# First SwiGLU block: the output of the last 1024 inner features as seven-product units whose operands lie in the room of the input's

## Chip, core and metric

The kernel runs on one core of a Trainium2 chip. The metric is the device time of one execution in microseconds (us). The kernel before takes 1906.6 us (median of three runs, 1905.49 to 1906.69). The engines are named as in the profile: PE multiplies matrices, DVE and ACT work on vectors, POOL adds and issues some transfers, SP issues most transfers.

## What is computed

One layer of a streaming encoder on 576 frames (512 of a prompt, 64 of a sample): a SwiGLU block, a mixer of three branches, a second SwiGLU block, and a final norm.

```python
def swiglu(x, w_in, w_out):
    a, b = jnp.split(x @ w_in, 2, axis=-1)
    return (jax.nn.silu(a) * b) @ w_out

def layer(x, lp, st):
    h = x + 0.5 * swiglu(rmsnorm(x, lp['norm_ffn1']), lp['w_ffn1_in'], lp['w_ffn1_out'])
    mix, new_st = mixer(rmsnorm(h, lp['norm_mix']), lp, st)
    h = h + mix
    h = h + 0.5 * swiglu(rmsnorm(h, lp['norm_ffn2']), lp['w_ffn2_in'], lp['w_ffn2_out'])
    return h, new_st
```

The model has 1024 features, a block 4096 inner features, so `w_in` is 1024 x 8192 and `w_out` 4096 x 1024. The change concerns the last 1024 rows of `w_ffn1_out` alone: x += 0.5 * g[:, 3072:4096] @ w_ffn1_out[3072:4096, :].

## The kernel before

Features lie on the 128 partitions, frames along the free axis. A float32 operand is split into a high part in the matrix engine's reduced format (a cast on ACT, line 335) and the rest (a subtraction on DVE, line 336); a product is the sum of three matmuls, high x high, high x low, low x high. High and low are ph and pl for weights, TH and TL for the moving operands of the seven-product form, YH and YL (XH and XL in the mixer) for those of plain products.

**Seven products.** Most of the layer uses one step of Strassen's scheme (Winograd's form) over a unit: 1024 rows of weights in two halves of 512, two output tiles of 128 features, and the frames in two halves of 288. A unit takes seven products instead of eight; one is 4 depth steps x 3 terms = 12 matmuls of 288 columns (`product`, line 714). They are named X1, A11, X3, X4, A22, A21, X2 after their weights. X1, X2, X3, X4 are sums of weight blocks: a transfer from POOL's queue adds two blocks in wx, and POOL adds a third block for X3 and for X4 (line 561). Blocks come as 256 KB tiles wr on SP's queue. Rings limit how far this runs ahead: five wr, four wx, six ph, six pl. `stream` puts out the units one after the other; in the slot of unit n stand X1, A11, X3, X4 of n between A22, A21, X2 of n-1. X1, A22, X3 and X2 of a unit share one accumulator bank, X4 and A21 another, A11 has one for all units; each product is read out of its bank by DVE or ACT before the next on that bank starts.

**The block.** `ffn` takes the inner features in four chunks c of eight tiles j. An input unit (c, j) makes one tile of both halves of `w_in` and turns them into g, 128 x 2 x 288 (`swiglu`, lines 725 to 741). An output unit (c, m) multiplies the g of chunk c with two column tiles of `w_out` and adds the results to the residual x, which is R (`residual`, line 753). Its moving operands are made from pairs of g tiles by `hidden_operands`: seven casts, seven TL and five differences of 288 columns (line 762) for each of four pairs. They stand in T2; the input's own operands stand in T, which has the same size. `tick` hands out one of the pieces at each product.

The order of units is: (0, 4..7); then for c = 1, 2, 3 the input units (c, 0), (c, 1), the four output units of chunk c-1, and (c, 2..7). After the stream the last chunk's output is plain: `hidden_parts` has split its g tiles into YH and YL, and `gemm` multiplies two blocks of 512 rows (i in (6, 7)) with four blocks of 256 columns, frames in halves of 256 and 320 (line 280); the second block does the first 256 frames of most columns before the other 320. Results are added to R at line 812. Then R is stored to `xs`, and the mixer begins: `norm` scales R into XH and XL (lines 392, 393), sums squares (lines 343 to 347), takes the root (line 352) and spreads it into rs with small transposes (line 385); its first plain products use XH and XL, their results are multiplied with rs (line 698), and `operands` makes xk and its differences from R and rs (from line 512).

The order of instructions on each engine is set by the framework's list scheduler, which places what a line emits by readiness in its own model; accumulator reads have a raised priority. Each engine then executes its own list strictly in order.

Of the kernel before, what the change touches and what calls it, by code (L numbers as in the profile page):

```python
# [26 lines left out]
F32 = mybir.dt.float32  # L27
# [6 lines left out]
TP = 512  # L34
HALVES = ((0, 256), (256, 320))
CH = [(0, 128), (128, 128), (256, 128), (384, 128), (512, 64)]
NB = 63
NS = 115
FH = 288
NPLAIN = 4  # L40
BUFS = {"g": 9, "t": 5, "P": 4, "Q": 2, "bias": 2}
# [1 line left out]
FBUFS = {"P": 5, "g": 5, "s": 3}  # L43
# [42 lines left out]
class Hybrid:  # L86
    def __init__(self, ctx, tc, I, O):
        self.tc, self.nc, self.I, self.O = tc, tc.nc, I, O
        self.op = None
        self.stay = {}  # L90
        self.plan = []
        self.splan = []
        self.ahead = {}
        self.steps = None
        self.b_i, self.b_n, self.fetched = 0, 0, deque()
        self.evicted = {}
        self.behind = 0
        self.jobs, self.gap, self.side = deque(), 0, iter(())
        nc = self.nc
        self.const = ctx.enter_context(tc.tile_pool(name="const", bufs=1))  # L100
        self.dram = ctx.enter_context(tc.tile_pool(name="scr", bufs=1, space=bass.MemoryType.DRAM))
        c = self.const
        self.R1 = c.tile([128, 8, T], F32, name="R1")
        self.rs = c.tile([128, T], F32, name="rs")
        self.small = ctx.enter_context(tc.tile_pool(name="small", bufs=8, reuse_waits="tile"))

        self.wt = ctx.enter_context(tc.tile_pool(name="wt", bufs=1, reuse_waits="tile"))
        self.xs = self.dram.tile([128, 8, T], F32, name="xs")

        self.ys = [self.dram.tile([128, T], F32, name=f"ys{i}") for i in range(16)]  # L110
        self.gs = [self.dram.tile([128, T], F32, name=f"gs{i}") for i in range(24)]
        self.scr = self.dram.tile([24, T], F32, name="scr_rows")


    @contextmanager
# [639 lines left out]
                done()  # L755
        return on

    def hidden_operands(self, kk, b1, b2):

        nc = self.nc  # L760
        put = lambda src, t: self.split(src, *(v[:, kk, :] for v in self.T2[t]))
        sub = lambda o, one, two: nc.vector.tensor_tensor(o, one, two, op=ALU.subtract)  # L762
        (b11, b12), (b21, b22) = ((b[:, 0, :], b[:, 1, :]) for b in (b1, b2))
        put(b22, self.T_X1)
        yield 1
        for t, b in ((self.T_A11, b12), (self.T_X3, b11)):
            d = self.P((128, FH))
            sub(d, b, b22)
            put(d, t)
            yield 1  # L770
        put(b11, self.T_X4)
        yield 1
        for t, one, two in ((self.T_A22, b22, b21), (self.T_A21, b12, b11), (self.T_X2, b21, b11)):
            sub(one, one, two)
            put(one, t)
            yield 1
# [5 lines left out]
    def ffn(self, x, g0, win, wout, name, last=(0, 1)):  # L782
# [3 lines left out]
        nc = self.nc  # L786
# [26 lines left out]
            return go  # L813


        def at(c, j):
            return (8 * c + (j if c == 3 else j % 2 * 4 + j // 2)) * 128

        boxes = [{} for _ in range(NPLAIN)]
        tiles = []  # L820
# [27 lines left out]
        def flush():  # L848
# [3 lines left out]
            for c, j in sorted(got):  # L852
                if c == 3:
                    self.jobs.append(self.hidden_parts(j, got.pop((c, j))))
                elif j % 2 == 0 and (c, j + 1) in got:
                    self.jobs.append(self.hidden_operands(j // 2, got.pop((c, j)), got.pop((c, j + 1))))
                    if j == 6:
                        free[0] = False

        def unit(c, j):  # L860
            def done(g):
                got[c, j] = g
                flush()
            return (win, 0, 4096 + at(c, j), at(c, j)), self.T, self.swiglu(done)

        def out(c, m):
            def done():
                free[0] = True
                if c == 2:
                    self.hidden_tiles(name)  # L870
                flush()
            return (wout, 1024 * c, 256 * m, 256 * m + 128), self.T2, self.residual(x, m, done if m == 3 else None)

        for j, box in enumerate(boxes):
            got[0, j] = box["g"]
        flush()
        seq = [unit(0, j) for j in range(NPLAIN, 8)]
        for c in range(1, 4):
            seq += [unit(c, j) for j in range(2)] + [out(c - 1, m) for m in range(4)] + [unit(c, j) for j in range(2, 8)]
        order = ((0, self.T_X1), (1, self.T_A22), (0, self.T_A11), (1, self.T_A21), (0, self.T_X3), (1, self.T_X2),  # L880
                 (0, self.T_X4))
        self.stream(seq, order, lambda n: {self.T_X1: n % 3, self.T_A11: 3, self.T_X4: 4 + n % 2})
        self.drain()
        for i in (6, 7):
            tiles = [((wout, i * 512, 512, j * 256, 256), [(0, evac_o(2 * j)), (128, evac_o(2 * j + 1))])
                     for j in range(4)]
            n = 1 if i == 7 else 4
            self.gemm(tiles[:n], self.YH, self.YL, k0=(i % 2) * 4)
            self.gemm(tiles[n:], self.YH, self.YL, k0=(i % 2) * 4, half_major=True, order=last)
# [692 lines left out]
    def run(self):  # L1582
# [42 lines left out]
        with self.ffn_phase("c"):  # L1625
            self.norm(x, C_G2, self.YH, self.YL)
            self.ffn(x, C_G2, "w_ffn2_in", "w_ffn2_out", "c", last=(1, 0))
            self.norm_out(x, C_GF, (self.O["y0"], self.O["y1"]))
        assert (len(self.plan), len(self.splan)) == (NB, NS), (len(self.plan), len(self.splan))

    def branches(self, x):
# [48 lines left out]

_INS = {"xT": (1024, T), "wblk": (NB, 128, 1024), "sblk": (NS, 128, 2048), "cst": (128, C_N), "bias": (128, 8, 256), "ckT": (512, 512),
        "cv": (512, 512), "s0": (128, 1024), "mc0": (4, 128, 129)}
# [11 lines left out]
def pack(plans, inp):  # L1694
# [11 lines left out]
    w["gate"] = gate  # L1706
    wb = np.empty((NB, 128, 1024), f32)
    for i, (n, r0, nr, c0, ncol) in enumerate(plan):
# [61 lines left out]
```

## Time and profile before

| | |
|---|---|
| median of three runs | 1906.6 us (1905.49 to 1906.69) |
| profiled execution: time, span | 1904.78 us, 1903.0 us |
| granted clock of PE | 0.994 |
| busy: PE, DVE, ACT, POOL | 98%, 81%, 56%, 36% |
| first block's stream, first and last product | about 62 us, 525 us |
| its plain tail, between the stream's end and the mixer's first product | to 574.45 us |

Times in the trace are from the span's start. A row of the profile names the line, the engine, the operation, out<-in by the program's names and the shapes; "idle before" is idle time of that engine just before, with what ended it. A PE row is about 0.3 us long, but rows overlap: what a matmul costs is the time from one start to the next.

### The profile page before, as it was taken

How to read it: one execution, taken by the hardware profiler on the slowest of the kernel's cores; microseconds unless marked ns; L12 is line 12 of the kernel's file. 1: busy time of each engine (PE TensorE's matmuls, PEld its weight loads, DVE VectorE, ACT ScalarE, POOL GpSimd, SP SyncE). 2: the span in 40 equal slices, each digit the busy share in tenths (PEclk: the TensorE clock that was granted, in tenths of full speed). 3: DMA queues.
4: the chain of work that ended last, by engine and by line, in shares of the span. 5: the costliest groups of instructions: out<-in, count | busy, mean ns of one | idle time of the engine just before them, and what ended most of it. 6: DMA issues, size and time to landing. Idle time of an engine off the chain costs nothing. (4 is left out here: it accounts for less than half of the span.)

```text
span 1903.0 us, 37603 instructions
## 1 busy us (share of the span) xinstructions
PE 1860.0 (98%) x13901; PEld 1812.3 (95%) x13901; DVE 1538.0 (81%) x2723; ACT 1070.9 (56%) x2406; POOL 685.6 (36%) x645
## 2 busy tenths in 40 slices
PE   9899999999999899999999999999999999999998
PEld 9899999999999779989899999999999999999997
DVE  7999999998858858767778776655899988889865
ACT  6554654554535677677676675334465554554544
POOL 3443343343301324523535453530344334333311
PEclk9999999999999999999999999999999999999999
DMA  7356666566643455755657655642446656656531
GB/s 222 107 155 167 163 158 173 156 165 167 178 132 111 128 156 157 213 164 132 189 156 188 177 157 187 212 154 75 122 115 167 173 156 166 166 157 169 148 100 56
DMA packets 129439, 294.69 MB, mean 155 GB/s; under 512 B 14288, under 2 KB 26192, under 8 KB 129256
## 3 DMA queue, kind: packets, MB, share of 16 engines
q1 hardware_dynamic: 99368, 203.42, 32.1%
q0 software_dynamic: 20272, 74.20, 20.7%
q10 hardware_dynamic: 9616, 14.69, 2.6%
q8 instruction: 109, 1.79, 0.4%
q14 instruction: 74, 0.61, 0.1%
HBM read 272.87 MB, written 19.38 MB: 154 GB/s over the span
## 5 line engine op out<-in xcount | busy, mean ns | idle before, releaser
L714 PE MATMUL acc<-TH,ph 128*128 128x288 f32 x3220 | 962.4, 300 | 18.4 <-ACT uv L622 5.5
L714 PE MATMUL acc<-TL,ph 128*128 128x288 f32 x3220 | 956.0, 297 | 1.3 <-DVE TL L336 1.1
L714 PE MATMUL acc<-TH,pl 128*128 128x288 f32 x3220 | 949.6, 296 | 0.6 <-DVE pl L336 0.6
L714 PEld LDWEIGHTS acc<-TH,ph 128*128 128x128 f32 x3220 | 605.1, 188 | 33.0 <-ACT uv L622 7.4
L714 PEld LDWEIGHTS acc<-TL,ph 128*128 128x128 f32 x3220 | 606.8, 188 | 5.6 <-issue 2.9
L714 PEld LDWEIGHTS acc<-TH,pl 128*128 128x128 f32 x3220 | 607.8, 189 | 1.8 <-DVE pl L336 1.1
L336 DVE TENSOR_TENSOR pl<-wr,ph 128x512 fp32r<-128x512 f32 x471 | 449.8, 961 | 83.1 <-ACT ph L335 71.4
L335 ACT CAST ph<-wr 128x512 fp32r<-128x512 f32 x471 | 287.5, 618 | 271.6 <-PE acc L714 146.3
L336 DVE TENSOR_TENSOR pl<-wx,ph 128x512 fp32r<-128x512 f32 x390 | 319.3, 822 | 32.6 <-ACT ph L335 26.8
L335 ACT CAST ph<-wx 128x512 fp32r<-128x512 f32 x390 | 237.6, 620 | 181.3 <-POOL wx L561 97.1
L561 POOL TENSOR_TENSOR wx<-wx,wr 128x512 f32<-128x512 f32 x160 | 246.2, 1539 | 179.2 <-DVE pl L336 143.9
L549 POOL DMA_DIRECT2D wx<-in_sblk x115 | 101.4, 915 | 497.9 <-DVE pl L336 186.0
L280 PE MATMUL acc<-YH,ph 128*128 128x256 f32 (+1 forms) x768 | 227.2, 298 | 2.4 <-ACT g L629 2.2
L280 PE MATMUL acc<-YL,ph 128*128 128x256 f32 (+1 forms) x768 | 227.4, 297 | 0.6 <-DVE YL L393 0.6
L280 PE MATMUL acc<-YH,pl 128*128 128x256 f32 (+1 forms) x768 | 227.1, 296 | 0.0
L280 PEld LDWEIGHTS acc<-YH,ph 128*128 128x128 f32 x768 | 145.2, 190 | 3.5 <-ACT g L629 2.3
L280 PEld LDWEIGHTS acc<-YL,ph 128*128 128x128 f32 x768 | 145.5, 189 | 1.1 <-DVE YL L393 1.0
L280 PEld LDWEIGHTS acc<-YH,pl 128*128 128x128 f32 x768 | 145.3, 189 | 0.0
L561 POOL TENSOR_TENSOR wy<-wx,wr 128x512 f32<-128x512 f32 x35 | 62.7, 1793 | 122.1 <-DVE pl L336 100.0
L753 DVE SCALAR_TENSOR_TENSOR R<-acc,R 128x288 f32<-128x288 f32 x168 | 75.7, 451 | 17.3 <-PE acc L714 16.3
L335 ACT CAST TH<-g 128x288 fp32r<-128x288 f32 x120 | 51.4, 433 | 49.5 <-POOL g L739 31.5
L739 POOL TENSOR_TENSOR g<-g,P 128x288 f32<-128x288 f32 x56 | 63.3, 1130 | 40.9 <-ACT P L738 40.8
(325 smaller groups left out, 2348.3 us busy)
## 6 DMA issues: line engine op xcount, KB each, us to landing
wr<-in_sblk SPq DMA_DIRECT2D x345, 256.0 KB, 3.6
wx<-in_sblk POOLq DMA_DIRECT2D x119, 512.0 KB, 6.5
wx<-in_sblk SPq DMA_DIRECT2D x111, 512.0 KB, 3.7
wr<-in_wblk SPq DMA_DIRECT2D x126, 256.0 KB, 3.0
R<-scr_rows ACTq DMA_DIRECT2D x12, 576.0 KB, 6.4
gs<-g SPq DMA_DIRECT2D x20, 288.0 KB, 3.5
g<-gs POOLq DMA_DIRECT2D x20, 288.0 KB, 3.6
y<-ys POOLq DMA_DIRECT2D x12, 288.0 KB, 5.2
```

The costliest lines, as they stand in the source:

```text
L280: last = nc.tensor.matmul(ps[:, :n], wt[:, wsl], xx[:, k0 + k, a:a + n], start=(k == 0 and i == 0), stop=(k == nk - 1 and i == 2))
L335: self.cast = self.nc.scalar.copy(hi, src).ins
L336: self.nc.vector.tensor_tensor(lo, src, hi.bitcast(F32), op=ALU.subtract)
L549: nc.gpsimd.dma_start(x12, src[:, 1:3, :], accum_op=ALU.add)
L561: add = lambda o, one, two: self.nc.gpsimd.tensor_tensor(o, one, two, op=ALU.add)
L714: self.nc.tensor.matmul(ps, wt[:, wsl], xx[:, kk, :], start=(start and kk == 0 and i == 0), stop=(kk == 3 and i == 2), skip_group_check=True)
L739: nc.gpsimd.tensor_tensor(s["g"][:, 1, :], s["g"][:, 1, :], a, op=ALU.mult)
L753: self.nc.vector.scalar_tensor_tensor(o, ps, scale, o, op0=ALU.mult, op1=ALU.add)
```

## The change

For the first block alone (`name == "a"`):

- All eight input units of chunk 3 stand ahead of the output units of chunk 2, and four output units (3, m) stand behind those. The tail of plain products is gone; the second block keeps it.
- The moving operands of chunk 3's output are made by `hidden_operands` too, written into T, when the input units no longer need it. The tiles j of this chunk are renumbered so that the pairs come out right.
- Five g buffers hold the tiles j = 3..7. The first three are stored to DRAM (hs) by SP and loaded back (`again`) when a buffer is free.
- In all, 55 weight blocks of the plain form and 119 of the seven-product form, where it was 63 and 115.

```diff
-    def hidden_operands(self, kk, b1, b2):
+    def hidden_operands(self, kk, b1, b2, to=None):
         nc = self.nc
-        put = lambda src, t: self.split(src, *(v[:, kk, :] for v in self.T2[t]))
+        put = lambda src, t: self.split(src, *(v[:, kk, :] for v in (to or self.T2)[t]))
...
+        seven = name == "a"
         def at(c, j):
-            return (8 * c + (j if c == 3 else j % 2 * 4 + j // 2)) * 128
+            if c == 3:
+                return (24 + ((6, 3, 7, 0, 4, 1, 5, 2)[j] if seven else j)) * 128
+            return (8 * c + j % 2 * 4 + j // 2) * 128
...
+        def again(i):
+            g = self.wp.tile([128, 2, FH], F32, name="g", tag="g", bufs=FBUFS["g"])
+            nc.sync.dma_start(g, self.hs[i])
+            return g
+
+        def last_operands(gs):
+            put = partial(self.hidden_operands, to=self.T)
+            yield from put(0, gs[0], gs[1])
+            g0, g1 = again(0), again(1)
+            yield from put(1, gs[2], gs[3])
+            g2 = again(2)
+            yield from put(2, gs[4], g0)
+            yield from put(3, g1, g2)
+        kept = []
         def unit(c, j):
             def done(g):
+                if c == 3 and seven:
+                    if j < 3:
+                        nc.sync.dma_start(self.hs[j], g)
+                    else:
+                        kept.append(g)
+                    if j == 7:
+                        self.jobs.append(last_operands(kept))
+                    return
                 got[c, j] = g
                 flush()
...
-            return (wout, 1024 * c, 256 * m, 256 * m + 128), self.T2, self.residual(x, m, done if m == 3 else None)
+            return ((wout, 1024 * c, 256 * m, 256 * m + 128), self.T if c == 3 else self.T2,
+                    self.residual(x, m, done if m == 3 and c < 3 else None))
...
-            seq += [unit(c, j) for j in range(2)] + [out(c - 1, m) for m in range(4)] + [unit(c, j) for j in range(2, 8)]
+            ins, outs = [unit(c, j) for j in range(8)], [out(c - 1, m) for m in range(4)]
+            seq += ins + outs + [out(3, m) for m in range(4)] if c == 3 and seven else ins[:2] + outs + ins[2:]
...
-        for i in (6, 7):
+        for i in () if seven else (6, 7):
```

How the instructions stand. DVE at the end of the last input unit, before (YL takes a g tile of chunk 3; line 812 is a plain result):

```order
L741 TENSOR_TENSOR g_6412<-acc_6399,P_6525 128x288
L336 TENSOR_TENSOR pl_6703<-wr_6700,ph_6702 128x512
L336 TENSOR_TENSOR YL_5949<-g_6412,YH_5948 128x576
L336 TENSOR_TENSOR pl_6765<-wr_6762,ph_6764 128x512
L733 TENSOR_TENSOR P_6648<-P_6648,acc_6531 128x288
L336 TENSOR_TENSOR pl_6771<-wr_6768,ph_6770 128x512
L812 SCALAR_TENSOR_TENSOR R1_60<-acc_6706,R1_60 128x256
```

and now, in the same place (lines are one higher; TL15, TL20, TL22 and the like are operands of chunk 3's output in T):

```order
L337 TENSOR_TENSOR pl_6113<-wx_5758,ph_6112 128x512
L337 TENSOR_TENSOR TL15_128<-g_5452,TH15_127 128x288
L337 TENSOR_TENSOR TL15_128<-g_5731,TH15_127 128x288
L763 TENSOR_TENSOR P_6274<-g_5452,g_5592 128x288
L763 TENSOR_TENSOR P_6296<-g_5452,g_5592 128x288
L763 TENSOR_TENSOR P_6432<-g_5731,g_5870 128x288
L337 TENSOR_TENSOR pl_6132<-wx_5619,ph_6131 128x512
L763 TENSOR_TENSOR g_5452<-g_5452 128x288
L763 TENSOR_TENSOR g_5592<-g_5592 128x288
L337 TENSOR_TENSOR TL20_130<-P_6274,TH20_129 128x288
L754 SCALAR_TENSOR_TENSOR R1_60<-acc_6135,R1_60 128x288
```

Pieces for the last output stand between the weights' low parts (pl) of chunk 2's output and in front of its additions to R.

SP in that stretch, now (hs are the stored tiles; wx and wr are weights of later units):

```order
L546 DMA wx_6174<-in_sblk 128x1024
L557 DMA wr_6168<-in_sblk 128x512
L867 DMA g_6408<-hs0_110 128x576
L557 DMA wr_6170<-in_sblk 128x512
L557 DMA wr_6172<-in_sblk 128x512
L867 DMA g_6410<-hs1_111 128x576
L867 DMA g_6566<-hs2_112 128x576
L546 DMA wx_6319<-in_sblk 128x1024
L557 DMA wr_6313<-in_sblk 128x512
```

The three loads stand in SP's queue between weights of the output units; before, only weights stood there.

DVE at the seam to the mixer, before, from the last addition to R (XL is the scaled residual, xd a sum of squares):

```order
L812 SCALAR_TENSOR_TENSOR R1_60<-acc_7224,R1_60 128x320
L393 SCALAR_TENSOR_TENSOR XL_7284<-R1_60,cst_143,XH_7283 128x320
L336 TENSOR_TENSOR pl_7474<-wr_7471,ph_7473 128x512
L347 TENSOR_TENSOR xd_7285<-xd_7285,xk_7291 128x256
L347 TENSOR_TENSOR xd_7285<-xd_7285,xk_7296 128x256
L393 SCALAR_TENSOR_TENSOR XL_7284<-R1_60,cst_143,XH_7283 128x320
L347 TENSOR_TENSOR xd_7285<-xd_7285,xk_7301 128x256
L347 TENSOR_TENSOR xd_7285<-xd_7285,xk_7306 128x256
```

and now:

```order
L754 SCALAR_TENSOR_TENSOR R1_60<-acc_7147,R1_60 128x288
L337 TENSOR_TENSOR pl_7532<-wr_7529,ph_7531 128x512
L394 SCALAR_TENSOR_TENSOR XL_7342<-R1_60,cst_146,XH_7341 128x256
L348 TENSOR_TENSOR xd_7343<-xd_7343,xk_7374 128x256
L348 TENSOR_TENSOR xd_7343<-xd_7343,xk_7379 128x256
L394 SCALAR_TENSOR_TENSOR XL_7342<-R1_60,cst_146,XH_7341 128x320
L348 TENSOR_TENSOR xd_7392<-xd_7392,xk_7398 128x320
L348 TENSOR_TENSOR xd_7392<-xd_7392,xk_7403 128x320
```

Before, all fourteen sums of squares stand behind the last addition; now five of the first half's seven stand ahead of it, and the second half's seven behind.

More of the change, by code (lines that the diff above doesn't have):

```diff
@@ L36 @@
 CH = [(0, 128), (128, 128), (256, 128), (384, 128), (512, 64)]
-NB = 63
-NS = 115
+NB = 55
+NS = 119
 FH = 288
@@ L112, in __init__ @@
         self.scr = self.dram.tile([24, T], F32, name="scr_rows")
+        self.hs = [self.dram.tile([128, 2, FH], F32, name=f"hs{i}") for i in range(3)]
     @contextmanager
@@ L868, in done @@
                 free[0] = True
-                if c == 2:
+                if c == 2 and not seven:
                     self.hidden_tiles(name)
                 flush()
-            return (wout, 1024 * c, 256 * m, 256 * m + 128), self.T2, self.residual(x, m, done if m == 3 else None)
+            return ((wout, 1024 * c, 256 * m, 256 * m + 128), self.T if c == 3 else self.T2,
+                    self.residual(x, m, done if m == 3 and c < 3 else None))
         for j, box in enumerate(boxes):
```

## The prediction

> **What bounds the kernel now.** The page first, then stretches and waits.
>
> ```profile
> span 1903.0 us, 37603 instructions
> PE 1860.0 (98%) x13901; PEld 1812.3 (95%) x13901; DVE 1538.0 (81%) x2723; ACT 1070.9 (56%) x2406; POOL 685.6 (36%) x645
> ```
>
> PE is busy 98%. Busy time over stretches (columns: length; busy time and count of PE, PEld, DVE, ACT, POOL; granted clock; DMA share; GB/s), first inside the first block's stream, then its plain tail, then the mixer's start:
>
> ```profile
> 412.00:512.00 100.00, 100.00 (x753) 100.00 (x752) 86.38 (x119) 52.00 (x97) 36.28 (x32) 1.00 0.64 167
> 526.00:574.00 48.00, 48.00 (x363) 48.00 (x363) 29.54 (x61) 16.93 (x31) 0.16 (x1) 1.00 0.44 130
> 575.00:593.00 18.00, 18.00 (x139) 17.78 (x138) 11.61 (x29) 10.05 (x24) 2.52 (x4) 1.00 0.32 100
> 593.00:622.00 29.00, 29.00 (x218) 28.99 (x217) 29.00 (x50) 13.43 (x25) 8.61 (x5) 1.00 0.28 100
> 622.00:636.00 14.00, 11.35 (x80) 9.78 (x79) 12.84 (x33) 9.40 (x20) 5.13 (x11) 1.00 0.41 138
> ```
>
> PE never pauses in stream and tail. DVE is at 86% in the stream, 62% in the tail, 100% from 593 to 622, and behind that PE runs 80 matmuls in 14 us. So PE bounds this block with DVE close behind. What PE waited for from 90.7 to 622 (us in all, times, longest):
>
> ```profile
> PE acc L714 <- ACT P L730: 2.2, 2, 2.0
> PE acc L714 <- DVE P L733: 0.7, 3, 0.3
> PE acc L714 <- ACT g L725: 0.3, 1, 0.3
> ```
>
> **Matmuls removed.** A stream matmul costs 100/753 = 0.1328 us, a tail one 48/363 = 0.1322. The tail has 2 x 4 x 2 x 2 x 4 x 3 = 384 (row blocks, column blocks, halves of a block, halves of the frames, depth, terms), 50.8 us; four units of seven products have 4 x 7 x 12 = 336, 44.6 us. PE saves **6.2 us**. A product is 12 x 0.1328 = 1.59 us.
>
> **DVE's new work.** Rows of the stream by form (count; busy, mean ns; idle before) of DVE, POOL and ACT:
>
> ```profile
> L336 DVE TENSOR_TENSOR pl<-wr,ph 128x512 fp32r<-128x512 f32 x115 | 139.5, 1223 | 11.2 <-ACT ph L335 8.1
> L336 DVE TENSOR_TENSOR pl<-wx,ph 128x512 fp32r<-128x512 f32 x152 | 122.7, 811 | 9.1 <-ACT ph L335 6.5
> L762 DVE TENSOR_TENSOR P<-g 128x288 f32<-128x288 f32 x21 | 20.8, 1028 | 0.0
> L561 POOL TENSOR_TENSOR wx<-wx,wr 128x512 f32<-128x512 f32 x75 | 112.9, 1505 | 71.5 <-DVE pl L336 56.5 <-issue 15.0
> L739 POOL TENSOR_TENSOR g<-g,P 128x288 f32<-128x288 f32 x27 | 31.0, 1147 | 9.2 <-ACT P L738 9.1
> L335 ACT CAST TH<-g 128x288 fp32r<-128x288 f32 x52 | 22.4, 433 | 25.1 <-POOL g L739 14.8 <-DVE g L741 7.2 <-DVE g L762 3.1
> ```
>
> Undisturbed, the same operations look like this (start, length):
>
> ```profile
> 401.70 0.45 DVE L336 TENSOR_TENSOR TL<-g,TH 128x288 fp32r<-128x288 f32 x1
> 402.07 0.45 DVE L762 TENSOR_TENSOR g<-g 128x288 f32<-128x288 f32 x1
> 402.44 0.68 DVE L336 TENSOR_TENSOR pl<-wx,ph 128x512 fp32r<-128x512 f32 x1
> 403.04 0.44 DVE L733 TENSOR_TENSOR P<-P,acc 128x288 f32<-128x288 f32 x1
> 403.40 0.45 DVE L336 TENSOR_TENSOR TL<-g,TH 128x288 fp32r<-128x288 f32 x1
> 415.63 3.06 DVE L336 TENSOR_TENSOR pl<-wr,ph 128x512 fp32r<-128x512 f32 x1
> ```
>
> Start to start, a 288-wide row takes 0.37 us (402.07 to 402.44) and a 512-wide one 0.60. The last row is a 0.68 us operation that took 3.06, for POOL was working:
>
> ```profile
> 415.79 1.59 POOL L561 TENSOR_TENSOR wx<-wx,wr 128x512 f32<-128x512 f32 x1
> 417.03 1.10 POOL L739 TENSOR_TENSOR g<-g,P 128x288 f32<-128x288 f32 x1
> ```
>
> DVE's excess over the undisturbed lengths is 115 x 0.54 + 152 x 0.13 + 21 x 0.58 = 94 us; POOL's additions and products are 112.9 + 31.0 = 143.9. So DVE loses 0.65 us per us of POOL while it often has nothing to do; with a full queue I take 0.8, bounds 0.65 and 1.0. The Trainium skill ("SBUF — State Buffer", section "SBUF: two separate sides") calls the port pair of these two engines an exclusive lock that is held for a whole instruction; by that every POOL addition would cost DVE its whole 1.5 us, and the sum below would end at -6.2 + 8.9 - 1.0 = +1.7, 1908.3 us. The 3.06 us row agrees with the rule, the 0.65 over the stream (there DVE often has a row from PSUM, or none) lies under it.
>
> The change orders 28 operand pieces on DVE as 48 rows of 288 (28 TL, 20 differences), where the eight 576-wide YL rows go. By the order almost all stand inside the output of chunk 2, 41 of them between the pl row of PE's sixth product (counted from product 1, the last input unit's X4) and that of the 22nd. That stretch has 76 DVE rows: 17 pl, and 59 narrow ones (41 pieces, 15 additions to R, 3 of swiglu). Bare, 17 x 0.60 + 59 x 0.37 = 32.0 us. With it run five additions and one g product on POOL, 5 x 1.505 + 1.147 = 8.7 us, so 7.0 more (5.7 to 8.7). The first TL15 row has to wait until product 1 has read that tile and ACT has cast: 1.6 us (0 where DVE is late anyway). DVE is through after 32.0 + 7.0 + 1.6 = 40.6 us; PE wants this pl at the start of product 22, after 21 x 1.59 = 33.4. The six buffers of ph and pl are already counted: DVE starts the stretch five products ahead. **PE stands 7.2 us** (from 32.0 + 5.7 - 33.4 = 4.3 to 32.0 + 8.7 + 1.6 - 33.4 = 8.9). Without the pieces, DVE would need 16.9 + 7.0 us for 17 products of 27.1.
>
> From there to the last product: 38 pl, 41 narrow, 13 rows of the norm (about 0.42 each by their neighbours) and some 11 POOL additions: 22.8 + 15.2 + 5.5 + 11 x 1.505 x 0.8 = 56.7 us of DVE for 38 x 1.59 = 60.4 of PE. No further wait, and little lead regained.
>
> **At nothing.** Three stores and three loads of g through SP: such transfers land within 3.6 us:
>
> ```profile
> gs<-g SPq DMA_DIRECT2D x20, 288.0 KB, 3.5
> g<-gs POOLq DMA_DIRECT2D x20, 288.0 KB, 3.6
> ```
>
> By the order 14 DVE rows (about 6 us) lie between the last reader of the buffer and the first reader of what is loaded into it. If that cover goes, DVE stops there and each us is PE's. Behind the waiting loads on SP stand weights of the unit after next, some ten products early. Stores wait for g on SP, ahead of weights that are as early. ACT gains 28 casts of 0.43 us and drops eight wide ones, at 52% in the stream. Weights: four blocks of sblk come for eight of wblk, at a DMA share of 0.64 against 0.44; no PE wait above names a DMA.
>
> **The seam to the mixer.** Now:
>
> ```profile
> 574.30 0.31 PE L280 MATMUL acc<-YH,pl 128*128 128x320 f32 x1
> 574.45 0.28 PE L280 MATMUL acc<-XH,ph 128*128 128x256 f32 x1
> 583.05 0.15 DVE L352 TENSOR_SCALAR sm<-ps_x 128x2 f32<-128x2 f32 x1
> 587.22 0.42 DVE L698 SCALAR_TENSOR_TENSOR g<-acc,rs 128x256 f32<-128x256 f32 x1 [0.53 <-ACT rs L409]
> 587.56 0.15 DVE L352 TENSOR_SCALAR sm<-ps_x 128x2 f32<-128x2 f32 x1
> 591.46 0.85 PE L385 MATMUL ps_x<-ident,sm 128*128 128x128 f32 x5
> 592.92 0.89 DVE L698 SCALAR_TENSOR_TENSOR g<-acc,rs 128x320 f32<-128x320 f32 x2 [1.53 <-ACT rs L409]
> 593.73 1.54 DVE L512 SCALAR_TENSOR_TENSOR xk<-R,cst,rs 128x576 f32<-128x576 f32 x2
> L392 ACT ACTIVATE XH<-R,cst 128x256 fp32r<-128x256 f32 x8 | 4.1, 510 | 6.5 <-DVE R L812 6.5
> L393 DVE SCALAR_TENSOR_TENSOR XL<-R,cst,XH 128x256 fp32r<-128x256 f32 x8 | 3.9, 482 | 2.1 <-ACT XH L392 2.1
> ```
>
> No gap on PE. The mixer's operands (xk) start 593.7 - 574.5 = 19.3 us into its first products and come late for PE, which loses 14 - 80 x 0.1328 = 3.4 us at 622 to 636. With the change the last features of both halves end together. Of the first mixer tile 18 matmuls (2.1 us) need none of them, and the last addition, XH and XL take 0.45 + 0.51 + 0.48 = 1.4, so PE goes on. Most squares are summed by then: by the order 14 rows (5.6 us at the rates above) lead from the last addition to the end of the sums, the first root being asked for at 4.6. From there to the first row that uses it is 4.2 us now (583.05 to 587.22), for the second 5.4 (587.56 to 592.92). So the second root is asked for near 9.5 and xk starts near 15, four us earlier, which can repay at most the 3.4. Against it, PE's transposes for the second root stand 100 matmuls (12.3 us) behind the seam, and their input is ready 3.9 us after it is asked for (587.56 to 591.46), at 13.4: 1.1 us of PE. I take **-1.0** (-3.4 to +1.1).
>
> **Sum:** -6.2 + 7.2 - 1.0 = 0.0; ends -5.3 and +3.8. The profiled execution's 1904.8 us stays 1904.8, and the median, 1.8 above it, 1906.6. I forecast **no change, 1906.5 us**, its own range 1903 to 1910.4. The measurement tells 0.2% (3.8 us) from none.
>
> **Rivals.** First, *the pieces hide.* DVE was 100% busy at 593 to 622 and PE missed nothing until 622; a full queue may lose no more to POOL than the 0.65, TL15's wait may vanish, and the seam repay in full: -6.2 + 4.3 - 3.4 = -5.3, 1901.3 us. Against it: all three at once. Chance 0.28 for anything beyond -3.8.
>
> Second, slower: *the wait turns into a slow clock.* PE's longest wait in this block was followed by half-speed matmuls (0.24 apart):
>
> ```profile
> 88.51 0.29 PE L714 MATMUL acc<-TH,pl 128*128 128x288 f32 x1
> 90.79 0.42 PE L714 MATMUL acc<-TH,ph 128*128 128x288 f32 x1 [1.98 <-ACT P L730]
> 91.03 0.43 PE L714 MATMUL acc<-TL,ph 128*128 128x288 f32 x1
> 90.00:95.00 5.00, 4.21 (x20) 4.21 (x21) 4.53 (x8) 3.16 (x9) 1.80 (x2) 0.66 0.50 159
> ```
>
> At 0.66 five us cost 1.7. If POOL blocks fully, a run of eight narrow rows between two pl leaves PE idle for 2 us at once near products 15 and 22: 8.9 us and two slow stretches of 1.7, with the late root 1.1: -6.2 + 8.9 + 3.4 + 1.1 = +7.2, 1913.8. It decides from a single gap of 2 us. Against it: at 622 to 636 PE lost 3.4 us in smaller gaps at clock 1.00. The Trainium skill ("TensorE: Matmul & The Clock Gate", section "What's actually happening") asks for an idle window of about 3.4 us before the clock halves; by that rule scattered waits leave it whole. The gap above was shorter and the clock fell, so the row decides. Chance 0.25 for slower than +3.8.
>
> Third, *only the matmuls count*: nothing waits, -6.2, 1900.4; it belongs to the first rival's 0.28.
>
> **Numbers.** No change 0.47, faster 0.28, slower 0.25. The range leaves out a tenth at each end: 1899.5 (all of the 6.2 and a us of seam) to 1912.5 (short of the second rival).
>
> **What would show it.** PE gaps of 6 to 9 us in all while chunk 2's output runs, ended by DVE's pl or R; DVE there at 97% or more; none in the last output; the first xk row 14 to 16 us after the first XH matmul; fewer waits behind the mixer's first products. I am wrong if PE runs through (faster), if the clock falls in that stretch or DVE waits for the loads of hs (slower), or if the mixer shifts by more than its 3.4 us.

## The result: 8.4 us faster at first, 5.9 over four comparisons, and more of it behind the seam than in the block that was changed

| | before | changed |
|---|---|---|
| median of six runs | 1906.5 us (1905.5 to 1908.2) | 1898.1 us (1896.4 to 1900.9) |
| ratio, 95% interval | | 0.9961 (0.9949 to 0.9972) |
| profiled execution: time, span | 1904.8, 1903.0 us | 1900.6, 1898.8 us |

The kernel is faster by 0.4%. I had forecast no change, and the time lies below my range. (Ratios and their intervals are formed from all undisturbed runs, and differ a little from the quotients of the medians.) The two traces differ by only 4.2 us, the medians by 8.4. So the first question is which parts of a trace can be trusted.

The changed kernel's page, head and busy times:

```profile
span 1898.8 us, 37636 instructions
PE 1854.9 (98%) x13853; PEld 1804.7 (95%) x13853; DVE 1561.7 (82%) x2771; ACT 1078.4 (57%) x2438; POOL 699.8 (37%) x657
```

Busy time over stretches of the changed kernel (columns as before: length; busy time and count of PE, PEld, DVE, ACT, POOL; granted clock; DMA share; GB/s): ahead of chunk 2's output, that output, the last output, then the mixer at two places:

```profile
412.00:474.00 62.00, 62.00 (x468) 62.00 (x467) 51.19 (x66) 35.35 (x74) 25.41 (x23) 1.00 0.69 183
474.00:526.00 52.00, 49.62 (x357) 47.52 (x356) 52.00 (x104) 26.09 (x57) 15.56 (x13) 1.00 0.53 149
526.00:573.00 47.00, 47.00 (x355) 47.00 (x354) 45.73 (x80) 27.05 (x51) 14.76 (x13) 1.00 0.81 215
...
621.00:636.00 15.00, 11.48 (x84) 10.46 (x83) 12.04 (x36) 8.97 (x22) 5.41 (x14) 0.99 0.40 133
```

DVE is now busy without a break while chunk 2's output runs, and PE does 357 matmuls there in the time of 392 (52 / 0.1327). What PE waited for from 90.7 to 620.4 us:

```profile
PE acc L715 <- ACT P L731: 2.7, 3, 2.4
PE acc L715 <- DVE pl L337: 1.2, 1, 1.2
PE acc L715 <- DVE P L734: 0.8, 3, 0.3
PE acc L715 <- DVE R L754: 0.5, 1, 0.5
```

The pl and R rows are new; the view names only part of what the rows' starts show, since a stop of 0.3 to 0.8 us between two matmuls is also followed by one matmul of 0.24 us. The first products of the mixer and the first xk, changed:

```profile
573.19 0.28 PE L281 MATMUL acc<-XH,ph 128*128 128x256 f32 x1
...
588.83 1.54 DVE L513 SCALAR_TENSOR_TENSOR xk<-R,cst,rs 128x576 f32<-128x576 f32 x2
```

XH starts 1.26 us earlier than before. The rest of the trace's gain comes behind it, and not at 621 to 636, where PE is busy 11.5 of 15 us (before 12.35).

**All traces side by side.** Each row is one trace, in us, from the starts of PE's rows: the first 2988 matmuls of the seven-product stream, and what stands between them; the 756 matmuls from there to the first XH matmul (708 with the change); from there until 288 seven-product matmuls of the mixer are done, until 300, and until 396; and from there to the end. The 62 to 63 us ahead of the stream are in no column. The letters are those of the experiments below.

| trace | 2988 | 756 or 708 | to 288 | to 300 | to 396 | rest | span |
|---|---|---|---|---|---|---|---|
| before | 411.3 | 100.5 | 109.6 | 10.2 | 24.6 | 1184.3 | 1903.0 |
| before again (I) | 411.6 | 100.5 | 109.6 | 11.1 | 24.5 | 1184.6 | 1904.3 |
| changed | 411.9 | 99.1 | 109.0 | 7.7 | 24.1 | 1184.7 | 1898.8 |
| changed again (A) | 412.5 | 99.3 | 109.0 | 7.6 | 22.6 | 1186.3 | 1900.0 |
| changed again (J) | 411.1 | 100.6 | 110.8 | 7.8 | 22.6 | 1185.7 | 1901.2 |
| pieces handed out early (F) | 414.2 | 99.3 | 107.4 | 7.7 | 24.1 | 1186.2 | 1901.6 |
| no pieces (B) | 413.1 | 94.3 | 109.0 | 7.6 | 24.1 | 1185.4 | 1896.0 |
| TL twice (C) | 413.9 | 107.2 | 109.3 | 7.7 | 22.6 | 1187.4 | 1910.6 |
| before, columns in both tails (D) | 411.4 | 100.5 | 108.3 | 7.6 | 22.6 | 1188.6 | 1901.3 |
| before, columns in the first tail (E) | 413.4 | 100.5 | 108.5 | 7.6 | 22.6 | 1184.3 | 1899.0 |
| the same again (K) | 412.1 | 100.5 | 108.4 | 7.6 | 22.6 | 1189.1 | 1902.6 |
| before, scores first (H) | 412.6 | 100.5 | 110.4 | 7.6 | 22.6 | 1183.1 | 1899.4 |
| differences on POOL (L) | 411.6 | 109.4 | 108.9 | 7.6 | 22.6 | 1186.1 | 1908.5 |
| gates early (M) | 412.0 | 99.5 | 119.2 | 7.6 | 22.6 | 1187.9 | 1911.6 |

The first column is the same number of matmuls in all of them. The last six units in it are others with the change: input units (3, 2) to (3, 7), where it was the output units of chunk 2 and the input units (3, 2) and (3, 3). That makes no difference that these traces can tell: it takes 412.1 us on average in the six traces with the old order of units and 412.5 in the eight with the new one, and within the eight it varies by 3 us. The rest varies by 6, and by 4.8 between E and K, which are one kernel. One pair of spans therefore can't tell 4 us from 8. The changed stretch and the columns from the 288th to the 396th repeat to a us within one order, but for slow-clock events; the column to the 288th varies by 3.4. Over the four traces of the changed order (changed, A, J, F) the 708 matmuls take 99.6 us against 100.5, and from XH to the 396th it is 140.1 us against 144.8. That is 1.0 and 4.6 us, 5.6 in all. The four comparisons of medians for that order of instructions gave 8.4, 6.0, 5.5 and 3.7 us, 5.9 on average. So the changed stretches and the medians agree, and the first comparison was a high one: no stretch shows its other 2.8 us. (The whole spans of the four traces are only some 3 us under the two of before, for the first column and the rest took 2.2 us more in them, which is within what these vary by.)

### The profile page after: what moved, and what is told of

It reads as the page before. It is cut to its first block, busy times and chain, and to the rows that moved or that the text cites. A ratio compares the mean times of both kernels' runs of the same rounds, so it can differ in the third digit from the quotient of the medians.

```text
span 1898.8 us, 37636 instructions
## 1 busy us (share of the span) xinstructions
PE 1854.9 (98%) x13853; PEld 1804.7 (95%) x13853; DVE 1561.7 (82%) x2771; ACT 1078.4 (57%) x2438; POOL 699.8 (37%) x657
## 4 chain that ended last, share of the span: by engine, by line
PE 62%; DVE 5%; ACT 4%; issue 2%; POOL 1%; DMA 1%; ACTq 0%; DVEq 0%; POOLq 0%
PE acc L715 41%; PE acc L281 16%; DVE pl L337 2%; ACT ph L336 1%; DVE TL L337 1%; PE ps_v L1442 1%; PE ps_s L1416 0%; PE ps_s L1105 0%; PE ps_x L1086 0%; DVE g L763 0%; PE ps_v L1150 0%; PE ps_x L1452 0%; PE ps_s L1235 0%; DMA scr_rows<-R 0%; ACT g L1334 0%
## 5 line engine op out<-in xcount | busy, mean ns | idle before, releaser
L715 PE MATMUL acc<-TH,ph 128*128 128x288 f32 x3332 | 996.0, 300 | 21.3 <-ACT uv L623 6.1
L715 PE MATMUL acc<-TL,ph 128*128 128x288 f32 x3332 | 987.9, 297 | 0.4 <-DVE TL L337 0.4
L715 PE MATMUL acc<-TH,pl 128*128 128x288 f32 x3332 | 981.0, 295 | 1.8 <-DVE pl L337 1.8
L715 PEld LDWEIGHTS acc<-TL,ph 128*128 128x128 f32 x3332 | 627.4, 188 | 4.4 <-issue 3.0
L281 PE MATMUL acc<-YH,ph 128*128 128x320 f32 (+1 forms) x640 | 189.6, 298 | 2.6 <-ACT g L630 2.2
L281 PE MATMUL acc<-YL,ph 128*128 128x320 f32 (+1 forms) x640 | 189.7, 297 | 0.6 <-DVE YL L394 0.6
L281 PE MATMUL acc<-YH,pl 128*128 128x320 f32 (+1 forms) x640 | 189.3, 297 | 0.0
L281 PEld LDWEIGHTS acc<-YH,ph 128*128 128x128 f32 x640 | 121.1, 190 | 3.7 <-ACT g L630 2.3
L281 PEld LDWEIGHTS acc<-YL,ph 128*128 128x128 f32 x640 | 121.4, 190 | 1.1 <-DVE YL L394 1.0
L281 PEld LDWEIGHTS acc<-YH,pl 128*128 128x128 f32 x640 | 121.2, 190 | 0.0
L336 ACT CAST TH<-g 128x288 fp32r<-128x288 f32 x140 | 59.6, 433 | 56.4 <-POOL g L740 33.4
```

The lines of the kernel that those rows point to most:

```text
L281: last = nc.tensor.matmul(ps[:, :n], wt[:, wsl], xx[:, k0 + k, a:a + n], start=(k == 0 and i == 0), stop=(k == nk - 1 and i == 2))
L336: self.cast = self.nc.scalar.copy(hi, src).ins
L715: self.nc.tensor.matmul(ps, wt[:, wsl], xx[:, kk, :], start=(start and kk == 0 and i == 0), stop=(kk == 3 and i == 2), skip_group_check=True)
```

## Experiments

**A. The changed kernel again**, nothing edited.

> The changed kernel once more, nothing edited. In its first trace the span is 4.2 us shorter than in that of the kernel before, while the medians differ by 8.4. If the account of the two traces is right, a second trace has the same parts: PE loses about 5.1 us between products 2 and 60 of the output of chunks 2 and 3 (99.1 us for 708 matmuls that would take 94.0 at 0.1327), and the mixer up to its 396th seven-product matmul takes 3.4 us less than before. If the difference between trace and median lies in the change itself, these parts differ from trace to trace; if it lies elsewhere (the first input units, the second block), they are the same to 0.5 us and other stretches differ by 2 to 4 us. Median expected: 1898, 1896.5 to 1900.

1900.4 us against 1906.4, ratio 0.9965 (0.9953 to 0.9977). PE lost 5.35 us over the 708 matmuls (5.13 in the first trace). The mixer's part was as short or shorter. The parts that I had named differ from the first trace by no more than a slow product behind the 300th matmul (1.5 us, in the first trace alone); the stretches that the change doesn't touch differ by 0.6 and 1.6 us.

**B. No pieces.** Twenty-eight casts, 28 TL rows, 20 differences, and the stores and loads of hs are left out.

```diff
                 if c == 3 and seven:
-                    if j < 3:
-                        nc.sync.dma_start(self.hs[j], g)
-                    else:
-                        kept.append(g)
-                    if j == 7:
-                        self.jobs.append(last_operands(kept))
                     return
```

> The changed kernel without the making of the last output's operands: the 28 casts, 28 TL rows and 20 differences of chunk 3 are left out, and so are the three stores and loads of g; its output units multiply what the input left in T. Theory one, the pieces on DVE make PE stand: the 5.1 us between products 2 and 60 go to under 0.5, and the time falls to about 1893 (1898.1 - 5.1). By the 7.2 us of the prediction it would be 1891. Rival, the weights' side (ACT, POOL, more blocks of the sum form) makes PE stand: most of the 5.1 stays, 1897 to 1898.

1896.4 us, 4.0 under A on the same chip (5.1 expected); the 708 matmuls take 94.3 us, 0.4 over their bare time. The window of chunk 2's output:

```profile
480.00:526.00 46.00, 46.00 (x348) 46.00 (x347) 39.85 (x59) 18.45 (x30) 14.70 (x13) 1.00 0.61 166
```

PE never stops, DVE is at 87%. The weights' side is not the cause; the pieces cost PE the whole of what it lost. This run takes the rows on DVE and the traffic of hs away together; the next adds DVE rows alone.

**C. TL twice.**

```diff
+            for _ in range(times - 1):
+                nc.vector.tensor_tensor(lo, src, hi.bitcast(F32), op=ALU.subtract)
```

> The changed kernel with each of the 28 TL rows of chunk 3 computed twice, so 28 more rows of 288 columns on DVE at 0.37 us, 10.4 us in all, in the same stretch. Theory one, DVE is the bound there and each of its us is PE's: PE loses 5.1 + 8 to 10.4 = 13 to 15.5 us between products 2 and 60, and the time is 1906 to 1908.5. Rival, PE waits there for something else and DVE has slack: less than 3 us more, at most 1901.

1907.7 us, 7.3 over A. PE's loss over the 708 matmuls goes from 5.35 to 13.2, 7.9 us more for 10.4 us of rows:

```profile
480.00:526.00 46.00, 38.30 (x254) 37.62 (x253) 45.99 (x100) 20.10 (x44) 19.62 (x9) 0.89 0.53 140
...
PE acc L715 <- ACT ph L336: 3.5, 1, 3.5
PE acc L715 <- DVE pl L337: 2.8, 1, 2.8
```

DVE is the bound while chunk 2's output runs, and of the 10.4 us more that it gets, PE loses three quarters. The ACT wait leads back to DVE too: in this trace ACT's casts wait 16.5 us for POOL's sums wx between 480 and 530 us, and POOL's sums wait 13.2 us for pl rows of DVE between 474 and 530. Here the clock falls to 0.89 as well.

**D. The kernel before, last tail block by columns.** In the plain tail, the second block of 512 rows goes column block by column block with both frame groups together, as the changed kernel ends.

```diff
-            n = 1 if i == 7 else 4
+            n = 4
```

> The kernel before with one number changed: the last block of the plain tail goes column block by column block, both frame groups together (n = 4 for both blocks), in place of the first frames of most columns first. By the order of instructions, the mixer's PE then stands almost as in the changed kernel: its transposes for the gates come after 38 seven-product matmuls (before 60, changed 37). Theory one, the 3.4 us that the mixer gave come from this seam and not from the seven-product form: the time is 3 us less than before, about 1903.3, and the mixer's stretch up to its 396th seven-product matmul is 3 to 3.4 us shorter. Rival, the mixer's gain hangs on the form or on chance of the trace: 1906.5, no change. Second rival, the frame groups together bring a stall at the seam (the second root comes late): 1907 to 1908.

1907.0 us, ratio 1.0002 (0.9993 to 1.0010): nothing. But the trace splits this into two. From XH to the 396th matmul it takes 138.5 us, 5.8 less than before; and from the last tail's first matmul to the last of all it takes 68.1 us in place of 62.2, because the edit reached the second block's tail too, where the final norm of the first frames had been hidden behind the second. One statement in the expectation doesn't hold for this kernel: its gates stand after 60 matmuls as before, not 38; what moved up in PE's list are the attention's transposes (the first after 108, before 125) and the scores of the second attention unit.

**E and K. The same in the first block only.**

```diff
-            n = 1 if i == 7 else 4
+            n = 1 if i == 7 and name != "a" else 4
```

> The kernel before with the column order of the last run, but in the first block alone; the second block's tail keeps its first-frames-first order, which the last run lost at its end (68.1 us from the tail's start to the last matmul, 62.2 in all others). Theory one, the changed kernel's gain comes from how the mixer stands behind the new end of the block, not from the seven-product form: the mixer's stretch from the first XH matmul to the 396th seven-product one is 138.5 to 139.5 us as in the last run (before 144.3), the end is 62.2, and the median is 1901 to 1903. Rival, the shorter matmul work is what the median shows: 1906.4 within 2.

1901.2 us against 1905.8, ratio 0.9982 (0.9973 to 0.9990); again (K) 1901.9 against 1906.2, 0.9975 (0.9966 to 0.9984). One number in the kernel before, with no seven-product unit added, gives 4.3 to 4.6 us. From XH to the 396th it is 138.6 us within 0.1 in all three traces of this seam.

**J beside K.**

> The changed kernel beside the kernel before with the column order (next), on one chip, since its gain over before was 8.4, 6.0 and 3.7 us in three comparisons of one order of instructions. Theory one, the seven-product form itself brings what the first block's trace shows, 48 matmuls (6.4 us) less 5.1 us of standing, and the rest is the mixer's order: the changed kernel is 0 to 2 us under the next kernel, both 4 to 6 us under before. Rival, the form brings more than its trace shows: 3 us or more under the next kernel.

> The kernel before with the column order in the last block of the first tail, again, beside the changed kernel. Theory one: 0 to 2 us above the changed kernel, 4 to 6 under before, about 1901. Rival: 3 us or more above the changed kernel.

On one chip the changed kernel took 1900.7 us (0.9970, 0.9958 to 0.9982) and K 1901.9. The two intervals overlap, so this pair alone tells the 1.2 us neither from none nor from 3. With the 1.0 us that the traces show in the first block it fits theory one: the form itself is worth about a us, the seam the rest. The trace of J shows something else besides, told under the rivals below.

**H. Scores first.** What in the mixer is it? Here is PE in the kernel before, around the 288th seven-product matmul (rows of L714 between them left out; those at the end are the next product):

```profile
683.15 0.95 PE L1132 MATMUL ps_v<-Q,t 128*64 128x64 f32 x20
...
685.82 0.70 PE L1073 MATMUL ps_s<-g 64*128 64x256 f32 x4
686.45 0.44 PE L1054 MATMUL ps_x<-ident,P 128*128 128x128 f32 x2
687.30 0.44 PE L1118 MATMUL ps_v<-Q,t 128*64 128x128 f32 x4 [0.41 <-ACT Q L1058]
689.63 0.44 PE L1054 MATMUL ps_x<-ident,P 128*128 128x128 f32 x2 [1.89 <-ACT P L1045]
...
694.60 0.44 PE L714 MATMUL acc<-TL,ph 128*128 128x288 f32 x1
694.84 0.44 PE L714 MATMUL acc<-TH,pl 128*128 128x288 f32 x1
...
680.00:700.00 20.00, 16.52 (x119) 12.03 (x118) 9.55 (x30) 12.40 (x38) 2.54 (x2) 0.83 0.45 125
```

Twelve matmuls run first, then the second scores of the second attention unit (L1073, 256 columns a head), and right behind them, with only small work between, the transposes of what softmax makes of these scores (L1054 at 689.63). Softmax is a chain over DVE and ACT, and with nothing left to do PE waits 1.89 us for it. The next product runs at half speed (0.24 us from start to start), and the clock of the window is 0.83. In the changed kernel:

```profile
681.61 0.70 PE L1105 MATMUL ps_s<-g 64*128 64x256 f32 x4
...
683.94 0.38 PE L1086 MATMUL ps_x<-ident,P 128*128 128x128 f32 x2
685.35 0.44 PE L1086 MATMUL ps_x<-ident,P 128*128 128x128 f32 x2 [1.03 <-ACT Q L1090]
```

The scores stand ahead of the twelve matmuls, which cover most of the softmax. The list scheduler's order came out so with the change, and in D and E too. H raises the priority of that unit's first scores and their softmax in the kernel before:

```diff
-        Ps = scores(0)
+        with self.tc.high_priority(offset=EVAC) if i == 1 else nullcontext():
+            Ps = scores(0)
```

On PE this moves the second scores, which wait for the first, and nothing else up to the 396th matmul (twelve rows of L714 shown as one; on DVE and ACT a few neighbours of this softmax change places). Near 1178 us four plain matmuls change places too; the 110 matmuls around them take 18.4 us, as in both traces of before.

```
-L714 MATMUL acc<-TH,ph 128x288 ... twelve rows
 L1073 MATMUL ps_s<-g 128x256 x2
+L714 MATMUL acc<-TH,ph 128x288 ... twelve rows
 L1054 MATMUL ps_x<-ident,P 128x128 x2
```

> The kernel before with one raised priority in the mixer: the first two score products of the second attention unit. The order of instructions is that of before up to the 288th seven-product matmul of the mixer; there the two score matmuls stand ahead of the next twelve matmuls, as they do in the changed kernel, and not behind them. Nothing of the first block is changed. Theory one, this place is where the mixer gave its gain: from the 288th to the 300th seven-product matmul it takes 7.7 us in place of 10.2, the half-speed matmuls behind that wait go too (1.5 us more between the 300th and the 312th), and the median is 2.5 to 4 us under before, 1902.5 to 1904. Rival, an earlier start of the mixer's operands is needed for it: no change, 1906.4.

1903.6 us against 1905.8, ratio 0.9990 (0.9982 to 0.9999). In the trace 4.5 us less than before from the 288th matmul to the 396th, and 0.8 more ahead of it. The window now:

```profile
680.00:700.00 20.00, 17.60 (x148) 13.91 (x147) 11.57 (x33) 15.19 (x44) 3.44 (x5) 1.00 0.57 161
```

So the place of two score instructions is worth 2 to 4 us, without a change in the first block. No earlier operand is needed for that. By the medians it is about half of what the seam gave in E; which other places gave the rest was not tested one by one. (The expectation speaks of the first scores; the pair that moves is the second.)

**I. The kernel before again.**

> The kernel before once more for a second trace. The wait of 2.2 us behind the 288th seven-product matmul of the mixer hangs on the order of instructions, so it is there again (10.2 us from the 288th to the 300th), and the first block takes 511.8 us within 0.5 from the stream's start to the first XH matmul. If either was chance, it differs.

The wait is there again (11.1 us to the 300th), with more of the slow clock:

```profile
680.00:700.00 20.00, 16.78 (x112) 11.61 (x111) 8.79 (x29) 12.01 (x37) 2.53 (x2) 0.74 0.46 125
```

It is a property of the order, not of one execution. The first block took 512.15 us (511.82).

**F. Pieces handed out early**, when the last input unit but one is done.

```diff
-            yield from put(0, gs[0], gs[1])
+            for i, gap in enumerate(put(0, gs[0], gs[1])):
+                yield 2 if i == 5 else gap
...
-                    if j == 7:
+                    if j == 6:
                         self.jobs.append(last_operands(kept))
```

> The changed kernel with the operand pieces of chunk 3 starting when the last input unit but one is done, seven products earlier, each still one product apart (one step of two, so that no operand is overwritten before its product). Theory one, PE stands because DVE is full while chunk 2's output runs: DVE has about 14% idle in the seven products before (11.1 us), 1.5 us, and the pieces end seven products earlier, when the queue can refill: PE loses 2 to 3.5 us in place of 5.1, and the time is 1.5 to 3 us under the changed kernel's, 1896 to 1898 beside its 1898 to 1900. Rival, the pieces only move the stand to an earlier place: no difference.

1902.1 us against 1905.8, ratio 0.9984 (0.9975 to 0.9993), and PE loses 5.3 us as before. The scheduler put every instruction of every engine where it had been: where a piece is handed out in the program doesn't decide its place. So the cure was not tested; what F gives is one more comparison of the same order.

**L. Differences on POOL.**

```diff
-        sub = lambda o, one, two: nc.vector.tensor_tensor(o, one, two, op=ALU.subtract)
+        sub = lambda o, one, two: (eng or nc.vector).tensor_tensor(o, one, two, op=ALU.subtract)
```

> The changed kernel with the 20 differences of chunk 3 on POOL in place of DVE. DVE has 20 rows of 0.37 us fewer (7.4 us); POOL gets 20 operations of about 1.1 us (its own 288-column products take 1.08 to 1.15), 22 us. In the stretch where DVE is full, six POOL operations of 8.5 us cost it 4.5 us, 0.53 of their time. By that share DVE loses 11.7 us and wins 7.4: PE stands 9.4 us in place of 5.1, 4 us slower than the changed kernel. If POOL blocks DVE for all of its time: 14.6 us more, about 1913. If POOL's narrow operations cost DVE nothing, the 5.1 go to under 1 and it is 4 to 5 us faster than the changed kernel.

1910.5 us, ratio 1.0025 (1.0016 to 1.0034), 9.8 over J; PE loses 15.4 us over the 708 matmuls. The window of chunk 2's output, groups on DVE and POOL from 474.9 to 513 us, and what PE waited for:

```profile
480.00:526.00 46.00, 34.96 (x235) 34.32 (x234) 45.66 (x65) 20.47 (x45) 27.73 (x27) 0.89 0.52 133
...
L337 DVE TENSOR_TENSOR TL<-g,TH 128x288 fp32r<-128x288 f32 x15 | 13.8, 934 | 0.3 <-ACT TH L336 0.3
L337 DVE TENSOR_TENSOR TL<-P,TH 128x288 fp32r<-128x288 f32 x8 | 10.0, 1256 | 0.0
L754 DVE SCALAR_TENSOR_TENSOR R<-acc,R 128x288 f32<-128x288 f32 x11 | 4.9, 445 | 0.0
...
L763 POOL TENSOR_TENSOR g<-g 128x288 f32<-128x288 f32 x12 | 11.8, 1067 | 0.0
L763 POOL TENSOR_TENSOR P<-g 128x288 f32<-128x288 f32 x8 | 8.8, 1114 | 2.4 <-DMA g<-hs 2.4
...
PE acc L715 <- DVE R L754: 11.0, 2, 6.9
```

DVE's 13 pl and 37 narrow rows there would take 21.5 us bare; with 0.3 of idle time they took 38.1, so POOL's 27.6 us (with its additions and a product) cost 16.3, a share of 0.59. Beside the 4.4 us that POOL costs in the changed kernel (below) that is some 12 more, and 7.4 us of rows are gone: net 4 to 5, as expected by the share. PE lost 10 more than in A, 9 more than in J. The rest came in two long waits for R's additions, which stand behind slow TL rows in DVE's list, and at a lower clock behind these waits (the first row of the fence); I have not taken these two apart.

**M. Gates early.**

```diff
-            self.side = chain((None, None), self.gates(pre))
+            self.side = chain((None,), self.gates(pre))
```

> The changed kernel with the mixer's gate steps handed out one product earlier (one None ahead of them in place of two). Only the order in the mixer's first 288 seven-product matmuls changes; the first scores of the second attention unit stay ahead of the twelve matmuls behind the 288th. Theory one, that place alone gave the mixer's gain, and the order ahead of it is worth at most 1 to 2 us either way: the stretch from the first XH matmul to the 396th stays at 138.5 to 141, the time within 2 us of the changed kernel. Rival, the position of the gates is what counts: 3 us or more of difference.

1910.4 us, ratio 1.0015 (1.0005 to 1.0025), 9.8 over J. The stretch from XH to the 288th matmul takes 119.2 us in place of 107.4 to 110.8. My theory that order there is worth 1 to 2 us falls. PE waits for a softmax of the first attention unit, and the softmax for ACT's queue:

```profile
668.00 0.33 ACTq L190 DMA_DIRECT2D R<-scr_rows  x1
668.36 0.62 ACT L336 CAST ph<-wy 128x512 fp32r<-128x512 f32 x1 [4.74 <-DMA scr_rows<-R]
668.89 0.61 ACT L1077 ACTIVATE P<-P,sm 128x384 f32<-128x384 f32 x1
...
669.55 0.90 PE L1086 MATMUL ps_x<-ident,P 128*128 128x128 f32 x3 [5.63 <-ACT P L1077]
```

The gates store rows to DRAM, and ACT issues the load that brings them back spread out (L190). With the gates earlier, that load stands in ACT's list ahead of the softmax, and ACT stands for 4.74 us until the store has landed. In the changed kernel the same wait is there, 2.5 us long, at a place where PE has other work. So E, H and M point to one thing: what the mixer takes hangs on which small instruction stands ahead of which. From XH to the 396th matmul it is 138.6 us in E, 140.6 in H, 144.3 and 145.2 before and 149.4 in M.

## Why the prediction was wrong

**Matmuls removed: right.** 48 fewer at 0.1327 us are 6.4 us (forecast 6.2).

**DVE's new work: right in kind, too large.** PE lost 5.1, 5.35, 5.3 and 6.6 us over the 708 matmuls in the four traces, not 7.2, all within the ends that I gave (4.3 to 8.9). B and C show that the cause is the one named. The changed kernel's DVE and POOL from the end of the sixth product's pl (474.92) to that of the 22nd (510.73):

```profile
L337 DVE TENSOR_TENSOR TL<-g,TH 128x288 fp32r<-128x288 f32 x14 | 7.8, 577 | 0.0
L337 DVE TENSOR_TENSOR pl<-wx,ph 128x512 fp32r<-128x512 f32 x10 | 6.7, 679 | 0.0
L754 DVE SCALAR_TENSOR_TENSOR R<-acc,R 128x288 f32<-128x288 f32 x15 | 6.4, 445 | 0.0
L763 DVE TENSOR_TENSOR g<-g 128x288 f32<-128x288 f32 x11 | 5.6, 532 | 0.0
L337 DVE TENSOR_TENSOR pl<-wr,ph 128x512 fp32r<-128x512 f32 x6 | 5.2, 862 | 0.0
...
L562 POOL TENSOR_TENSOR wx<-wx,wr 128x512 f32<-128x512 f32 x5 | 7.5, 1491 | 11.8 <-DVE pl L337 9.2 <-issue 2.6
L740 POOL TENSOR_TENSOR g<-g,P 128x288 f32<-128x288 f32 x1 | 1.1, 1078 | 2.2 <-ACT P L739 2.2
```

There are 16 pl and 59 narrow rows, 31.4 us bare (forecast 32.0), and no idle time: the wait for TL15 (1.6) was not there. The stretch lasts 35.8 us (40.6), so POOL's 8.6 us cost 4.4 and not 7.0, a share of 0.51 and not 0.8. Against that, the stretch began 2.4 us later than I had counted: I let DVE end the sixth pl when PE starts product 1 (472.51). So 2.4 + 35.8 - 33.4 = 4.8 us are lost by product 22. The lead came back to 6 us by the 39th product, sooner than I thought.

**At nothing: right.** DVE has no idle time in the stretch, so the loads of hs came in time for it; ACT's casts waited once, 1.6 us, for one of them. B, without them, shows nothing that DVE's rows don't explain.

**The seam to the mixer: the step that failed.** I had allowed it -1.0 us, at most -3.4; it gave -4.6 on average (-3.2 to -6.0 between single traces). The first half of the step was right: xk starts 588.83 - 573.19 = 15.6 us after XH (forecast 15), and the second root did not hold PE up at all (forecast 1.1). The second half was wrong. I set the limit at what PE loses from 622 to 636 us, as if an earlier xk could be repaid only there, and had named a shift beyond 3.4 us as a sign of being wrong. By the 84th seven-product matmul the changed kernel is later, at 66.8 us from XH against 64.1; it is level at the 288th, and gains 2.4 to 3.5 us in the next twelve and up to 2 in the product behind them. What the change at the seam moved is the list scheduler's order of the mixer's instructions, up to 110 us behind the seam. I had compared the orders there only as far as the sums of squares. That such a gain needs no xk four us earlier shows in E, where the first XH matmul starts at 576.04:

```profile
594.34 1.54 DVE L512 SCALAR_TENSOR_TENSOR xk<-R,cst,rs 128x576 f32<-128x576 f32 x2
```

That is 18.3 us behind XH, one us sooner than before (19.3), and the mixer gains more than in the changed kernel. In H xk is as late as before.

**The sum.** Forecast -6.2 + 7.2 - 1.0 = 0.0; by the traces' means -6.4 + 5.4 - 4.6 = -5.6 (5.6 us lost, less the 0.2 lost there before), and the medians' mean is -5.9, which is 1900.6 us, inside my range. Of the miss to these -5.6, 1.8 us are DVE's term and 3.6 the seam's.

**The rivals.** "The pieces hide" named a time (1901.3) near what came on average, with 4.3 for the pieces and 3.4 for the seam; its reason for the seam, a full repayment of the waits at 622 to 636, is not what happened. "Only the matmuls count" falls, for PE stood; that its 1900.4 is what came on average is luck, the standing and the seam nearly cancelling. "The wait turns into a slow clock" shows in J: a single wait of 1.92 us, and half clock behind it:

```profile
502.60 0.40 PE L715 MATMUL acc<-TH,pl 128*128 128x288 f32 x1 [1.92 <-DVE pl L337]
...
502.00:508.00 6.00, 5.40 (x29) 5.40 (x30) 6.00 (x13) 0.00 (x0) 1.60 (x1) 0.72 0.50 153
```

There PE lost 6.6 us over the 708 matmuls; in the first trace the same place had a wait of 1.17 us and the clock stayed at 1.00. The slow matmuls cost 6 x 0.28 = 1.7 us there; at the end of the 708 PE's loss is 1.3 to 1.5 us above that of the other three traces, the longer wait included. So that rival's trigger was sound and its price a little high, and it fired at this place in one trace of four.

## What to carry to other kernels

When a list scheduler sets the order, an edit moves instructions far behind the place that it touches; compare the orders as far as they differ, and look for an engine's instruction that stands right behind the start of a chain that it needs the end of, and for a transfer that waits in the list of an engine with urgent work. Before crediting a gain to a new form of a computation, make its side effect alone: here one number in the old kernel gave 4.3 to 4.6 us where the whole change gave 5.9, and two score instructions about 2. A single pair of traces can't be summed to a time when the unchanged stretches vary by 3 and 6 us; compare the stretches.

## What the runs showed of the hardware

**POOL slows DVE rows that read two operands from SBUF, and not those that read one from PSUM.** Over the kernel before, additions to R in the seven-product units, which read one operand from PSUM (the accumulators) and one from SBUF (the tiles' memory), never take more than 460 ns, as long as undisturbed, while pl rows do:

```profile
L753 DVE SCALAR_TENSOR_TENSOR R<-acc,R 128x288 f32<-128x288 f32 x168 | 75.7, 451 | 17.3 <-PE acc L714 16.3
L336 DVE TENSOR_TENSOR pl<-wr,ph 128x512 fp32r<-128x512 f32 x471 | 449.8, 961 | 83.1 <-ACT ph L335 71.4 <-PE acc L280 1.8 <-DMA out_c<-cs 0.7
```

In L the R rows stay at 445 ns beside TL rows at 934 and 1256. So 18 of the 59 narrow rows in my stretch could not be slowed, and I had priced all alike. The Trainium skill ("SBUF — State Buffer", section "SBUF: two separate sides") states just this condition, a DVE operation with two SBUF inputs against a GpSimd operation that reads SBUF; the traces agree. Its lock for a whole instruction would put the price at up to POOL's full time; with DVE idle for 0.3 us at most it was 0.51 (changed) and 0.59 (L). A row that has begun is held up too: the prediction's row of 3.06 us began 0.16 us ahead of POOL, and was 2.4 us longer than undisturbed, about the 2.3 us from POOL's start to the end of its second operation.

**Half clock after less than 2 us, and not each time.** Half-speed matmuls followed waits of 1.89 (before) and 1.92 us (J). Just behind the 300th matmul the changed order lost 1.5 us to it in two traces of four, with the same waits ahead of it in all four (0.9 to 1.1, 0.46 and 1.08 us within the 5 us before). The Trainium skill ("TensorE: Matmul & The Clock Gate", section "What's actually happening") puts the change behind an idle window of about 3.4 us that runs freely and does not start with the kernel. That a window's phase decides would fit two out of four; that it has to be idle for 3.4 us does not fit the waits.
